# Affine part of a reloaded residual on VectorE by halves, more zero matmuls at the start, and high passes first, in a two-layer decoder trunk

## The chip, the cores and the metric

The kernel runs on one core of a Trainium2 chip. The metric is device time in microseconds (us) of one execution. The engines of the core are TensorE (PE: matmuls and transposes, and PEld, its weight load), VectorE (DVE), ScalarE (ACT) and GpSimd (POOL); SyncE (SP) issues most transfers. Matmul results land in PSUM, all else lies in SBUF.

## The reference

Input and output are 512 tokens (S) by 1024 channels (D), float32. After a first layer norm come two equal layers:

```python
for l in range(DEPTH):                       # DEPTH = 2
    proj = h @ w_in[l]
    cq, ckv, kr, xp, xqk, xv, xo, ipre, fpre = jnp.split(proj, ...)
    a = mla(cq, ckv, kr, ...)                # attention, 4 heads
    p = multiscale_pool(xp, ...)
    m = mlstm(xqk, xv, xo, ipre, fpre, ...)
    mix = jnp.concatenate([a, p, m], axis=-1) @ w_out[l]
    h = layer_norm(ALPHA * h + mix, ln1_g[l], ln1_b[l])
    f = conv_glu_ffn(h, w_up[l], w_fconv[l], b_fconv[l], w_down[l])
    h = layer_norm(ALPHA * h + f, ln2_g[l], ln2_b[l])
```

## The kernel before

**Tiles and products.** The tokens stand in NT = 4 tiles of 128, the channels in KD = 8 groups of 128 ("k-tiles"). Each float32 operand is split into a high part (rounded to fp32r) and a low part (the rest), and each product is three matmuls: hi times hi, hi times lo, lo times hi. Weights are streamed. `fetch` (L145 on) issues the transfer of one piece of at most 1024 columns into a raw buffer (of 2), lets ScalarE copy it to hi (L158) and one engine, named piece by piece in the table of `add_w`, subtract for lo (L159: VectorE or GpSimd); hi and lo have 4 buffers each. `getw` fetches at most one piece ahead of the one in use. Names carry the piece: lo_o_1_2 is the low part of quarter 2 of half 1 of w_out, and the quarters are taken in that order.

**Order.** TensorE's order is written by generators that a planner runs, each by its readiness and modelled time; the other engines' instructions are ordered by a scheduler that goes by priority.

**Opening.** x comes in by tiles. TensorE multiplies zeros (wz, L381) 14 times. `first_norm` makes each tile's statistics and normalised value, writes it to DRAM (`spill`, L230) without gain and bias, and transposes it (L239, tp_in, in two halves of four k-tiles); ScalarE applies gain and bias (L244), and `split` makes a_hi (L178) and a_lo (L179). `tm_gemm` then computes the projection ia tile by tile over six k-tiles, three matmuls (L290, L291, L292) for each in a row: x hi by weight hi, x hi by weight lo, x lo by weight hi. After it runs the remaining two k-tiles as further groups.

**Attention.** The q, k and v projections are evacuated by VectorE: qn, qp (with its rotary steps, L737 to L741, and L722), kn, v (L179). Softmax takes a maximum (L783), and pr (L789) is transposed (L806, pt). Meanwhile the lo parts of uq_1 and of all of half 0 of w_out are made on GpSimd.

**Output projection and residual.** The attention's pool is closed; `spill` is read back as h, four 128x1024 tiles, GpSimd multiplies by the gain gb_p (L885) and VectorE adds the bias (L886). w_out runs in two column halves (`out_gen`): half 0 with one chunk in its last group, half 1 with three, so that tile after tile is completed over chunks 1, 2 and 3. `resid` evacuates half a tile: h = ALPHA h + psum (L834) and its statistics (L193). After half 1 `ln_tail` normalises, writes to `spill` (in the last layer to the output), transposes and splits; the gain and bias of ln1, g1, are applied to h on GpSimd during the feed-forward part (`ln_affine`).

**Feed-forward and tail.** `t_half` runs the first three up pieces over token tiles 0 and 1, then 2 and 3; `t_one` the others. The down projection is again a `tm_gemm` in two halves, its last group three chunks long in half 1. In the last layer `ln_tail` ends in the output: subtract mean and multiply by gain (L210), multiply by rs and add bias (L224, VectorE), the last tile by halves; for tile 2 ScalarE multiplies (L212) and GpSimd adds (L217). rs comes from GpSimd's power (L190).

Of the kernel before, what the change touches and what calls it, by code (L numbers as in the profile page):

```python
# [13 lines left out]
AF = mybir.ActivationFunctionType  # L14
ALU = mybir.AluOpType
# [3 lines left out]
P = 128  # L19
# [76 lines left out]
def trunk(ctx: ExitStack, tc: tile.TileContext, I: dict, out: bass.AP, layers=DEPTH):  # L96
# [33 lines left out]
    def mmc(n):  # L130
        return n / 2400.0 + 0.003
# [66 lines left out]
    def ln_tail(pool, h, i, st, gb, cols, name, transpose=True, dst=None, pre=1.3):  # L198
# [6 lines left out]
        if not transpose:  # L205
            n = D // 2 if i == NT - 1 else D
            with ExitStack() as hs:
                if i == NT - 1:
                    hs.enter_context(tc.high_priority(offset=1000))
                V.scalar_tensor_tensor(z, z, mv[:, 0:1], gb[:, 0, :], ALU.subtract, ALU.mult)  # L210
                if i == NT - 2:
                    A.activation(z, z, AF.Copy, scale=rs[:, 0:1])  # L212
                    for a in range(0, D, D // 2):
                        if a:
                            yield 0.0, 0.0, "rs_end"
                            hs.enter_context(tc.issue_after(last_rs[0]))
                        G.tensor_add(z[:, a : a + D // 2], z[:, a : a + D // 2], gb[:, 1, a : a + D // 2])  # L217
                        A.dma_start(dst[i * P : (i + 1) * P, a : a + D // 2], z[:, a : a + D // 2])
                    return
                if i == NT - 1:  # L220
                    sch.set("rs_end")
                for a in range(0, D, n):
                    za = z[:, a : a + n]
                    V.scalar_tensor_tensor(za, za, rs[:, 0:1], gb[:, 1, a : a + n], ALU.mult, ALU.add)  # L224
                    nc.sync.dma_start(dst[i * P : (i + 1) * P, a : a + n], za)
# [34 lines left out]
    def tm_gemm(chunks, n, stat, evac, name, nlast=1, nfirst=1, waits=None, twaits=None):  # L260
# [7 lines left out]
        for g in groups:  # L268
# [11 lines left out]
            for i in range(NT):  # L280
                if twaits and done == 0:
                    yield 0.0, 0.0, twaits[i]
                at = done
                for (hi, lo), kts in loaded:
# [25 lines left out]
    def t_half(names, waits):  # L310
        ws, os_ = [], []
        for hf in range(2):
# [3 lines left out]
            for n, nm in enumerate(names):  # L316
# [5 lines left out]
                for k in range(KD):  # L322
                    mm3(os_[n][:, t0 * P : t1 * P], hi[:, k * P : (k + 1) * P], lo[:, k * P : (k + 1) * P],
                        a_hi[:, t0:t1, k, :], a_lo[:, t0:t1, k, :], k == 0, k == KD - 1)
                    if k % 2 == 1:
                        yield 6 * mmc(256), 0.0, None
# [22 lines left out]
    for l in range(layers):  # L349
# [12 lines left out]
        add_w(I["w_uq"][l, 1], 6 * P, f"uq{l}_1", G)  # L362
        for half in range(2):
            for q in range(4):
                add_w(I["w_out"][l, half, q], 1024, f"o{l}_{half}_{q}", G if half == 0 else V)
# [14 lines left out]
    for i in range(14):  # L380
        T.matmul(wp, wz[:, :P], wz, start=True, stop=True)  # L381
# [18 lines left out]
    def first_norm():  # L400
        for i in range(NT):
# [3 lines left out]
            yield from ln_tail(lp, h, i, st, None, cols0, "in0", dst=spill)  # L405

# [634 lines left out]
```

## Time and profile before

| | before |
|---|---|
| median of 3 runs | 1184.91 us (1182.11 to 1185.75) |
| the profiled execution | 1184.34 us |
| its span | 1182.5 us |
| TensorE busy | 1139.6 us, 96% |
| VectorE busy | 631.4 us, 53% |
| ScalarE busy | 471.0 us, 40% |
| GpSimd busy | 265.1 us, 22% |
| granted TensorE clock, mean | 0.987 |

The span runs from the first to the last recorded instruction. Busy time is the union of an engine's instructions. [...] Line numbers (L159) are of the kernel before, and PSUM tiles carry the name of what is computed (o: output projection).

### The profile page before, as it was taken

The numbers are of one execution on the slowest core, as the hardware profiler recorded it, in microseconds if no ns is written. First come the engines' busy times: TensorE is split into PE (matmuls) and PEld (weight loads), VectorE is DVE, ScalarE is ACT, GpSimd is POOL, SyncE is SP. The second block draws the span as 40 slices with busy tenths as digits, with TensorE's granted clock in tenths as the row PEclk, the third lists the DMA queues.
The fourth block names the chain that finished last, engine by engine and source line by source line (L and its number), as shares of the span: only waits on it lengthen the run. The fifth ranks groups of instructions, "written<-read, shape, count | busy, mean of one in ns | idle before, by whom it ended". The sixth has DMA issues, their size and how long they took to land.

```text
span 1182.5 us, 14079 instructions
## 1 busy us (share of the span) xinstructions
PE 1139.6 (96%) x5426; PEld 948.4 (80%) x5426; DVE 631.4 (53%) x975; ACT 471.0 (40%) x815; POOL 265.1 (22%) x202
## 2 busy tenths in 40 slices
PE   7999999799999999999999999979999999999996
PEld 5878878688888888888887887868888888888885
DVE  6766885754543444223368579676544533432325
ACT  6564542453333333221267545417433333331120
POOL 0316613013331111000003363040334211110002
PEclk8999999899999999999999999989999999999998
DMA  7331214233243232323243112152323433332321
GB/s 291 103 104 60 85 37 160 89 108 104 92 131 101 90 106 89 104 92 94 96 154 125 63 50 89 53 180 58 113 98 107 125 99 97 93 104 89 107 72 71
DMA packets 35074, 120.76 MB, mean 102 GB/s; under 512 B 4408, under 2 KB 4920, under 8 KB 35008
## 3 DMA queue, kind: packets, MB, share of 16 engines
q1 hardware_dynamic: 34720, 119.35, 31.3%
q8 instruction: 42, 0.69, 0.2%
q10 hardware_dynamic: 288, 0.52, 0.1%
q14 instruction: 24, 0.20, 0.1%
HBM read 113.55 MB, written 6.31 MB: 101 GB/s over the span
## 4 chain that ended last, share of the span: by engine, by line
PE 76%; DVE 13%; POOL 4%; issue 2%; ACT 2%; DMA 1%; SPq 0%; POOLq 0%; DVEq 0%; ACTq 0%
PE t_up L173 13%; PE t_up L175 13%; PE t_up L174 13%; PE d L292 6%; PE d L290 6%; PE d L291 6%; PE o L291 1%; PE o L292 1%; PE o L290 1%; PE ia L292 1%; DMA h<-spill 1%; DVE qp L722 1%; PE ia L291 1%; PE ia L290 1%; POOL py L532 1%
## 5 line engine op out<-in xcount | busy, mean ns | idle before, releaser
L173 PE MATMUL t_up<-a_hi,hi_up 128*128 128x512 f32 (+1 forms) x752 | 282.7, 376 | 0.0
L174 PE MATMUL t_up<-a_lo,hi_up 128*128 128x512 f32 (+1 forms) x752 | 282.6, 376 | 0.0
L175 PE MATMUL t_up<-a_hi,lo_up 128*128 128x512 f32 (+1 forms) x752 | 282.3, 375 | 0.0
L159 DVE TENSOR_TENSOR lo_up<-raw_up,hi_up 128x1024 fp32r<-128x1024 f32 x88 | 120.6, 1371 | 162.5 <-ACT hi_up L158 159.4
L158 ACT CAST hi_up<-raw_up 128x1024 fp32r<-128x1024 f32 x88 | 92.8, 1054 | 182.7 <-PE t_up L174 170.2
L175 PEld LDWEIGHTS t_up<-a_hi,lo_up 128*128 128x128 f32 x752 | 141.5, 188 | 25.8
L174 PEld LDWEIGHTS t_up<-a_lo,hi_up 128*128 128x128 f32 x752 | 141.5, 188 | 25.8 <-DVE a_lo L179 0.2
L173 PEld LDWEIGHTS t_up<-a_hi,hi_up 128*128 128x128 f32 x752 | 141.5, 188 | 25.3
L914 POOL TENSOR_TENSOR f_lo<-y,f_hi 128x512 fp32r<-128x512 f32 x44 | 77.4, 1760 | 366.6 <-ACT f_hi L913 366.6
L159 DVE TENSOR_TENSOR lo_d<-raw_d,hi_d 128x1024 fp32r<-128x1024 f32 x44 | 53.9, 1224 | 159.6 <-ACT hi_d L158 159.2
L290 PE MATMUL d<-hi_d,f_hi 128*128 128x512 f32 x352 | 137.1, 389 | 0.0
L292 PE MATMUL d<-hi_d,f_lo 128*128 128x512 f32 x352 | 136.9, 389 | 0.0
L291 PE MATMUL d<-lo_d,f_hi 128*128 128x512 f32 x352 | 136.9, 389 | 0.0
L158 ACT CAST hi_d<-raw_d 128x1024 fp32r<-128x1024 f32 x44 | 46.4, 1055 | 176.2 <-PE d L292 157.1
L291 PEld LDWEIGHTS d<-lo_d,f_hi 128*128 128x128 f32 x352 | 66.1, 188 | 13.8
L292 PEld LDWEIGHTS d<-hi_d,f_lo 128*128 128x128 f32 x352 | 66.1, 188 | 13.7
L290 PEld LDWEIGHTS d<-hi_d,f_hi 128*128 128x128 f32 x352 | 66.1, 188 | 13.6
L912 DVE TENSOR_TENSOR y<-y,t_up 128x512 f32<-128x512 f32 x44 | 30.3, 688 | 74.4 <-PE t_up L175 66.9
L908 ACT ACTIVATE y<-y 128x512 f32<-128x512 f32 x44 | 27.8, 632 | 101.4 <-DVE y L907 101.4
L907 DVE SCALAR_TENSOR_TENSOR y<-t_up,pp,y 128x511 f32<-128x511 f32 x88 | 65.6, 746 | 1.5
L291 PE MATMUL o<-lo_o,a_hi 128*128 128x512 f32 x128 | 52.1, 407 | 13.8 <-DVE lo_o L159 13.8
L190 POOL TENSOR_TENSOR rs_d<-rs_d,nhalf 128x1 f32<-128x1 f32 x8 | 8.3, 1036 | 233.5 <-DVE rs_d L189 233.5
(264 smaller groups left out, 1927.1 us busy)
## 6 DMA issues: line engine op xcount, KB each, us to landing
raw_up<-in_w_up_dram SPq DMA_DIRECT2D x88, 512.0 KB, 3.5
raw_d<-in_w_dn_dram SPq DMA_DIRECT2D x44, 512.0 KB, 3.4
raw_o<-in_w_out_dram SPq DMA_DIRECT2D x16, 512.0 KB, 3.5
raw_it<-in_w_it_dram SPq DMA_DIRECT2D x12, 512.0 KB, 3.4
spill<-h SPq DMA_DIRECT2D x8, 512.0 KB, 2.8
raw_ib<-in_w_ib_dram SPq DMA_DIRECT2D x8, 512.0 KB, 3.5
h<-spill SPq DMA_DIRECT2D x8, 512.0 KB, 7.5
raw_uq<-in_w_uq_dram SPq DMA_DIRECT2D x6, 384.0 KB, 3.0
```

The costliest lines, as they stand in the source:

```text
L158: A.copy(h_, r_)
L159: eng.tensor_tensor(l_, r_, h_.bitcast(F32), ALU.subtract)
L173: T.matmul(o, whi, xhi, start=start, stop=False)
L174: T.matmul(o, whi, xlo, start=False, stop=False)
L175: T.matmul(o, wlo, xhi, start=False, stop=stop)
L290: T.matmul(o, xhi, whi, start=at == 0, stop=False)
L291: T.matmul(o, xhi, wlo, start=False, stop=False)
L292: T.matmul(o, xlo, whi, start=False, stop=at == nk - 1)
L907: V.scalar_tensor_tensor(y[:, t:], o[:, : S - t], w(2 - t), y[:, t:], ALU.mult, ALU.add)
L908: A.activation(y, y, AF.Silu)
L912: V.tensor_mul(y, y, o)
L914: f_sub[0] = G.tensor_sub(fbox["lo"][:, f, :], y, fbox["hi"][:, f, :].bitcast(F32)).ins
```

## The change

Seven things, the order following the diff:

1. In the last layer all tiles' final steps are on VectorE; the last tile does both steps by halves, and its second half leaves by ScalarE's queue.
2. In `tm_gemm`, where the first group waits tile by tile (ia alone), four k-tiles at a time run all hi·hi matmuls, then all with the weight's lo, then all with a_lo.
3. `t_half` does the same by four k-tiles.
4. The lo of uq_1 and of quarters 2 and 3 of w_out's half 0 moves from GpSimd to VectorE.
5. 29 zero matmuls instead of 14, and 6 more behind the transposes of tile 0.
6. Gain and bias of the reloaded h are both applied on VectorE, by halves of 512 columns: half 0 of all tiles first, half 1 of a tile behind the evacuation of its half 0. The transfers of g1's gain and bias are asked for later.
7. The last group of the last layer's second down half has four chunks instead of three.

```diff
         if not transpose:
             n = D // 2 if i == NT - 1 else D
-            with ExitStack() as hs:
-                if i == NT - 1:
-                    hs.enter_context(tc.high_priority(offset=1000))
-                V.scalar_tensor_tensor(z, z, mv[:, 0:1], gb[:, 0, :], ALU.subtract, ALU.mult)
-                if i == NT - 2:
-                    A.activation(z, z, AF.Copy, scale=rs[:, 0:1])
-                    for a in range(0, D, D // 2):
-                        if a:
-                            yield 0.0, 0.0, "rs_end"
-                            hs.enter_context(tc.issue_after(last_rs[0]))
-                        G.tensor_add(z[:, a : a + D // 2], z[:, a : a + D // 2], gb[:, 1, a : a + D // 2])
-                        A.dma_start(dst[i * P : (i + 1) * P, a : a + D // 2], z[:, a : a + D // 2])
-                    return
-                if i == NT - 1:
-                    sch.set("rs_end")
+            with tc.high_priority(offset=1000 if i == NT - 1 else 0):
+                for a in range(0, D, n):
+                    za = z[:, a : a + n]
+                    V.scalar_tensor_tensor(za, za, mv[:, 0:1], gb[:, 0, a : a + n], ALU.subtract, ALU.mult)
                 for a in range(0, D, n):
                     za = z[:, a : a + n]
                     V.scalar_tensor_tensor(za, za, rs[:, 0:1], gb[:, 1, a : a + n], ALU.mult, ALU.add)
-                    nc.sync.dma_start(dst[i * P : (i + 1) * P, a : a + n], za)
+                    (A if a else nc.sync).dma_start(dst[i * P : (i + 1) * P, a : a + n], za)
             return
...
                     yield 0.0, 0.0, twaits[i]
                 at = done
+                if twaits and done == 0:
+                    ops = [(hi, lo, q, kt) for (hi, lo), kts in loaded for q, kt in enumerate(kts)]
+                    for a in range(0, len(ops), 4):
+                        for p_ in range(3):
+                            for hi, lo, q, kt in ops[a : a + 4]:
+                                w = (lo if p_ == 1 else hi)[:, q * 512 : q * 512 + n]
+                                T.matmul(ps[i][:, :n], stat(kt, i)[p_ == 2], w, start=a == p_ == 0 and kt == ops[0][3],
+                                         stop=False)
+                        yield 3 * len(ops[a : a + 4]) * mmc(n), 0.0, None
+                    at = len(ops)
+                    continue
...
                 hi, lo = ws[n]
-                for k in range(KD):
-                    mm3(os_[n][:, t0 * P : t1 * P], hi[:, k * P : (k + 1) * P], lo[:, k * P : (k + 1) * P],
-                        a_hi[:, t0:t1, k, :], a_lo[:, t0:t1, k, :], k == 0, k == KD - 1)
-                    if k % 2 == 1:
-                        yield 6 * mmc(256), 0.0, None
+                for k0 in range(0, KD, 4):
+                    for p_ in range(3):
+                        for k in range(k0, k0 + 4):
+                            T.matmul(os_[n][:, t0 * P : t1 * P], (lo if p_ == 1 else hi)[:, k * P : (k + 1) * P],
+                                     (a_lo if p_ == 2 else a_hi)[:, t0:t1, k, :], start=k == p_ == 0,
+                                     stop=k == KD - 1 and p_ == 2)
+                    yield 12 * mmc(256), 0.0, None
...
-        add_w(I["w_uq"][l, 1], 6 * P, f"uq{l}_1", G)
+        add_w(I["w_uq"][l, 1], 6 * P, f"uq{l}_1", V)
...
-                add_w(I["w_out"][l, half, q], 1024, f"o{l}_{half}_{q}", G if half == 0 else V)
+                add_w(I["w_out"][l, half, q], 1024, f"o{l}_{half}_{q}", G if half == 0 and q < 2 else V)
...
     wp = bank("wp")
-    for i in range(14):
-        T.matmul(wp, wz[:, :P], wz, start=True, stop=True)
+
+    def warm(n):
+        for _ in range(n):
+            T.matmul(wp, wz[:, :P], wz, start=True, stop=True)
+
+    warm(29)
...
             yield from ln_tail(lp, h, i, st, None, cols0, "in0", dst=spill)
+            if i == 0:
+                warm(6)
...
-                h, gb = hbox["h"], hbox[which]
...
                     V.scalar_tensor_tensor(z, z, ALPHA, ps, ALU.mult, ALU.add)
                     ln_stats(h, i, half, stt[i])
+                if half == 0 and which == "g1":
+                    hbox["pre"](i, 1)
                 if half == 1:
...
         for i in range(NT):
             nc.sync.dma_start(h[:, i, :], spill[i * P : (i + 1) * P, :])
-            G.tensor_mul(h[:, i, :], h[:, i, :], gp[:, 0, :])
-            V.tensor_add(h[:, i, :], h[:, i, :], gp[:, 1, :])
-        hbox.update(h=h, pool=hp, g1=load_gb(hp, I["ln1_g"][l], I["ln1_b"][l], "1"))
+
+        def pre_affine(i, half):
+            c_ = slice(half * 512, half * 512 + 512)
+            V.tensor_mul(h[:, i, c_], h[:, i, c_], gp[:, 0, c_])
+            V.tensor_add(h[:, i, c_], h[:, i, c_], gp[:, 1, c_])
+
+        for i in range(NT):
+            pre_affine(i, 0)
+        hbox.update(h=h, pool=hp, pre=pre_affine)
...
             ffn_open()
+            hbox["g1"] = load_gb(hp, I["ln1_g"][l], I["ln1_b"][l], "1")
...
-                                   f"d{half}", nlast=1 if half == 0 else 3))
```

VectorE at the junction of the output projection and the residual, first layer. The o_0 to o_3 at L834 (L842 in the new numbering) are the PSUM tiles of the four token tiles, h the reloaded residual, st_a its statistics, lo_o_1_2 and lo_o_1_3 the low weights of half 1. Before:

```order
L159 TENSOR_TENSOR lo_o_1_2_2044<-raw_o_1_2_2041,hi_o_1_2_2043 128x1024
L886 TENSOR_TENSOR h_1946<-h_1946,gb_p 128x1024 x2
L834 SCALAR_TENSOR_TENSOR h_1946<-h_1946,o_0_1694 128x512
L886 TENSOR_TENSOR h_1946<-h_1946,gb_p 128x1024
L193 BN_STATS st_a_1977<-h_1946 128x6
L834 SCALAR_TENSOR_TENSOR h_1946<-h_1946,o_1_1695 128x512
L834 SCALAR_TENSOR_TENSOR h_1946<-h_1946,o_2_1696 128x512
L193 BN_STATS st_a_1986<-h_1946 128x6
L193 BN_STATS st_a_1995<-h_1946 128x6
L834 SCALAR_TENSOR_TENSOR h_1946<-h_1946,o_3_1697 128x512
L159 TENSOR_TENSOR lo_o_1_3_2050<-raw_o_1_3_2047,hi_o_1_3_2049 128x1024
L193 BN_STATS st_a_2004<-h_1946 128x6
```

The changed kernel, the end of the same stretch:

```order
L193 BN_STATS st_a_2006<-h_1967 128x6
L899 TENSOR_TENSOR h_1967<-h_1967,gb_p 128x512
L842 SCALAR_TENSOR_TENSOR h_1967<-h_1967,o_2_1717 128x512
L898 TENSOR_TENSOR h_1967<-h_1967,gb_p 128x512
L193 BN_STATS st_a_2017<-h_1967 128x6
L899 TENSOR_TENSOR h_1967<-h_1967,gb_p 128x512
L842 SCALAR_TENSOR_TENSOR h_1967<-h_1967,o_3_1718 128x512
L898 TENSOR_TENSOR h_1967<-h_1967,gb_p 128x512
L193 BN_STATS st_a_2028<-h_1967 128x6
L899 TENSOR_TENSOR h_1967<-h_1967,gb_p 128x512
L159 TENSOR_TENSOR lo_o_1_2_2070<-raw_o_1_2_2067,hi_o_1_2_2069 128x1024
L159 TENSOR_TENSOR lo_o_1_3_2076<-raw_o_1_3_2073,hi_o_1_3_2075 128x1024
```

The low weights lo_o_1_2 and lo_o_1_3 stand together behind all multiplications (L898), additions (L899) and half-0 evacuations; before, lo_o_1_2 stood behind the first addition and lo_o_1_3 behind the last evacuation.

VectorE in the attention, first layer; the L722 rows (L730 in the new numbering) are the rotated q, and mx is the first maximum of a softmax. Before:

```order
L179 TENSOR_TENSOR v_1393<-uv_1369,v_1393 128x512
L722 TENSOR_TENSOR qp_1402<-qp_1287,qp_1402 64x512 x2
L179 TENSOR_TENSOR v_1407<-uv_1370,v_1407 128x512
L722 TENSOR_TENSOR qp_1416<-qp_1314,qp_1416 64x512 x2
L179 TENSOR_TENSOR v_1421<-uv_1371,v_1421 128x512
L179 TENSOR_TENSOR qn_1440<-uq_1_1430,qn_1440 128x512
L783 TENSOR_REDUCE mx<-s 128x1
```

The changed kernel:

```order
L179 TENSOR_TENSOR v_1414<-uv_1390,v_1414 128x512
L730 TENSOR_TENSOR qp_1423<-qp_1308,qp_1423 64x512 x2
L179 TENSOR_TENSOR v_1428<-uv_1391,v_1428 128x512
L730 TENSOR_TENSOR qp_1437<-qp_1335,qp_1437 64x512 x2
L179 TENSOR_TENSOR v_1442<-uv_1392,v_1442 128x512
L179 TENSOR_TENSOR qn_1461<-uq_1_1451,qn_1461 128x512
L159 TENSOR_TENSOR lo_o_0_2_1878<-raw_o_0_2_1875,hi_o_0_2_1877 128x1024
L791 TENSOR_REDUCE mx<-s 128x1
L159 TENSOR_TENSOR lo_o_0_3_1936<-raw_o_0_3_1933,hi_o_0_3_1935 128x1024
L792 TENSOR_SCALAR mx<-mx 128x1
```

The order of v and qp is the same; lo_o_0_2 and lo_o_0_3 come in around the first maximum. (The lo of uq_1 stands further ahead, between the two qn in front of the rotary steps.)

TensorE in the opening; ia_162 (ia_177 in the new one) is token tile 0's PSUM tile, hi_ia_0 to hi_ia_2 hold two k-tiles of the weight each, and tp_in are transposes. Before, from the transposes of tile 1 on:

```order
L239 MATMUL tp_in_200<-ident,h_92 128x128 x4
L239 MATMUL tp_in_212<-ident,h_92 128x128 x4
L290 MATMUL ia_162<-hi_ia_0_121,a_hi 128x456
L291 MATMUL ia_162<-lo_ia_0_122,a_hi 128x456
L292 MATMUL ia_162<-hi_ia_0_121,a_lo 128x456
L290 MATMUL ia_162<-hi_ia_0_121,a_hi 128x456
L291 MATMUL ia_162<-lo_ia_0_122,a_hi 128x456
L292 MATMUL ia_162<-hi_ia_0_121,a_lo 128x456
L290 MATMUL ia_162<-hi_ia_1_127,a_hi 128x456
L291 MATMUL ia_162<-lo_ia_1_128,a_hi 128x456
L292 MATMUL ia_162<-hi_ia_1_127,a_lo 128x456
```

The changed kernel, from the same transposes to those of tile 2:

```order
L228 MATMUL tp_in_221<-ident,h_92 128x128 x4
L228 MATMUL tp_in_233<-ident,h_92 128x128 x4
L279 MATMUL ia_177<-hi_ia_0_136,a_hi 128x456 x2
L279 MATMUL ia_177<-hi_ia_1_142,a_hi 128x456 x2
L279 MATMUL ia_177<-lo_ia_0_137,a_hi 128x456 x2
L279 MATMUL ia_177<-lo_ia_1_143,a_hi 128x456 x2
L279 MATMUL ia_177<-hi_ia_0_136,a_lo 128x456 x2
L279 MATMUL ia_177<-hi_ia_1_142,a_lo 128x456 x2
L279 MATMUL ia_177<-hi_ia_2_148,a_hi 128x456 x2
L279 MATMUL ia_177<-lo_ia_2_149,a_hi 128x456 x2
L279 MATMUL ia_177<-hi_ia_2_148,a_lo 128x456 x2
L228 MATMUL tp_in_273<-ident,h_92 128x128 x4
```

Where a_lo was asked for by the third matmul, it is asked for by the ninth; the last two k-tiles of the group follow as two more triples of passes.

## Rows read from the trace of the kernel before

**Rows 1.** The page's busy times: us, share of the span, instructions.
```profile
PE 1139.6 (96%) x5426; PEld 948.4 (80%) x5426; DVE 631.4 (53%) x975; ACT 471.0 (40%) x815; POOL 265.1 (22%) x202
```
**Rows 2.** TensorE's waits: who, for whom: us in total, times, longest us.
```profile
PE o L291 <- DVE lo_o L159: 13.8, 2, 6.9
...
PE s L173 <- DVE v L179: 3.4, 2, 1.7
```
**Rows 3.** Windows: us, PE, PEld, DVE, ACT, POOL busy, PEclk, DMA share, GB/s.
```profile
210.00:220.00 10.00, 5.47 (x14) 4.33 (x15) 8.37 (x14) 0.00 (x0) 0.55 (x1) 0.66 0.59 206
```
**Rows 4.** Timeline, TensorE, opening: start, us, operation, [idle before <- releaser].
```profile
1.25 4.79 PE L381 MATMUL wp<-wz 128*128 128x512 bf16 x14 [1.25 <-DVE wz L378]
9.46 1.09 PE L239 MATMUL tp_in<-ident,h 128*128 128x128 f32 x8 [3.42 <-DVE h L228]
...
13.42 0.48 PE L290 MATMUL ia<-hi_ia,a_hi 128*128 128x456 f32 x1 [1.60 <-ACT a_hi L178]
...
16.33 0.75 PE L292 MATMUL ia<-hi_ia,a_lo 128*128 128x456 f32 x1 [2.22 <-DVE a_lo L179]
...
22.12 1.03 PE L239 MATMUL tp_in<-ident,h 128*128 128x128 f32 x8
```
**Rows 5.** Timelines of ScalarE and VectorE, opening.
```profile
17.57 0.62 ACT L178 CAST a_hi<-lnt_in 128x512 fp32r<-128x512 f32 x1
...
19.53 0.64 DVE L179 TENSOR_TENSOR a_lo<-lnt_in,a_hi 128x512 fp32r<-128x512 f32 x1
```
**Rows 6.** Timeline of VectorE, attention of the first layer.
```profile
136.32 0.68 DVE L741 TENSOR_TENSOR qp<-qp,qp 128x512 f32<-128x512 f32 x1
136.92 0.69 DVE L737 TENSOR_TENSOR qp<-uq,cs 128x512 f32<-128x512 f32 x1
...
141.04 0.96 DVE L741 TENSOR_TENSOR qp<-qp,qp 128x512 f32<-128x512 f32 x1
...
145.03 3.50 DVE L722 TENSOR_TENSOR qp<-qp,qp 64x512 fp32r<-64x512 f32 x2
...
149.29 2.77 DVE L722 TENSOR_TENSOR qp<-qp,qp 64x512 fp32r<-64x512 f32 x2
```
**Rows 7.** Timeline of GpSimd, the same stretch.
```profile
145.41 2.57 POOL L159 TENSOR_TENSOR lo_o<-raw_o,hi_o 128x1024 fp32r<-128x1024 f32 x1 [3.96 <-ACT hi_o L158]
```
**Rows 8.** Timeline of TensorE, behind that stretch.
```profile
154.98 0.30 PE L806 MATMUL pt<-ident,pr 128*128 128x128 f32 x1 [0.22 <-DVE pr L789]
```
**Rows 9.** Chain of waits, 186 to 245 us: start, us on the chain, what.
```profile
187.95 6.29 DMA h<-spill
...
219.17 0.43 PE o L292
...
219.87 0.23 PE o L291
```
**Rows 10.** Timeline of VectorE, junction of the first layer.
```profile
200.16 3.41 DVE L159 TENSOR_TENSOR lo_o<-raw_o,hi_o 128x1024 fp32r<-128x1024 f32 x1
...
208.56 1.21 DVE L886 TENSOR_TENSOR h<-h,gb_p 128x1024 f32<-128x1024 f32 x1
...
213.27 1.21 DVE L159 TENSOR_TENSOR lo_o<-raw_o,hi_o 128x1024 fp32r<-128x1024 f32 x1
```
**Rows 11.** Timeline of TensorE, junction and first up projection.
```profile
214.53 0.80 PE L291 MATMUL o<-lo_o,a_hi 128*128 128x512 f32 x1 [6.85 <-DVE lo_o L159]
...
232.97 0.36 PE L173 MATMUL t_up<-a_hi,hi_up 128*128 128x256 f32 x1
```
**Rows 12.** Timelines of VectorE and GpSimd, tail.
```profile
1163.63 1.28 DVE L224 SCALAR_TENSOR_TENSOR h<-h,rs_d,gb 128x1024 f32<-128x1024 f32 x1 [0.44 <-POOL rs_d L190]
...
1174.15 0.15 DVE L189 TENSOR_SCALAR rs_d<-mv_d 128x1 f32<-128x1 f32 x1
1174.21 1.26 POOL L217 TENSOR_TENSOR h<-h,gb 128x512 f32<-128x512 f32 x1 [1.26 <-ACT h L212]
...
1177.00 2.40 DVE L224 SCALAR_TENSOR_TENSOR h<-h,rs_d,gb 128x512 f32<-128x512 f32 x2 [0.44 <-POOL rs_d L190]
```

More of the change, by code (lines that the diff above doesn't have):

```diff
@@ L826, in f @@
             def f(i, ps):
-                h, gb = hbox["h"], hbox[which]
+                h, gb = hbox["h"], hbox.get(which)
                 if half == 0:
@@ L940, in ffn_main @@
                                          dst=out if last else spill),
-                                   f"d{half}", nlast=1 if half == 0 else 3))
+                                   f"d{half}", nlast=1 if half == 0 else 4 if last else 3))
             if not last:
```

## The prediction

> **What bounds the kernel now.** The page's first part comes first: TensorE is busy 1139.6 of 1182.5 us, every other engine at most 53% [rows 1]. So the end moves only by what TensorE idles, by what it runs at the lower clock, and by what follows its last matmul. The list of TensorE's waits is next: by far the largest is for a lo weight of the output projection, 13.8 us in two waits, one a layer; 3.4 us go to the attention's v, again in two [rows 2]. The opening and the tail are read from the timelines. The profiled run took 1184.34 us, span 1182.5; the sum is made against 1184.34. The median, 1184.91, is 0.6 above it. A measurement of this kernel can tell about 0.3%, 3.5 us, from no change.
>
> **Opening.** The 14 zero matmuls take 4.79 us from 1.25 on; then TensorE idles 3.42 until the first transposes at 9.46 [rows 4]. A 512-column matmul takes 0.43 at the lower level of the clock and 0.23 at the higher one [rows 9], so 4.79 is about 8 of the first and 6 of the second. Fifteen more at 0.23 are 3.45: they end at 6.04 + 3.45 = 9.5, as the transposes become ready. If the clock rose later, 29 x 0.43 = 12.5 would end at 13.7 and hold them up. The six zeros behind tile 0's transposes (1.4 us) lie in the idle time before the first projection matmul, 1.60 long [rows 4]: no cost. Then TensorE waits again, 2.22 us for an a_lo, until 16.33, and that matmul takes 0.75 where the first one at 13.42 took 0.48 [rows 4]: the clock has fallen. With all hi passes of four k-tiles first, eight matmuls run before the first a_lo is asked for, so most of the 2.22 goes. What is late next is the data of tile 0's other half: a_hi at 17.57 + 0.62 = 18.2, a_lo at 19.53 + 0.64 = 20.2 [rows 5], and behind it two matmuls, some 20.6 where before the tile ended at 22.12 [rows 4]. That is 1.5; I take **-1.2**, as tile 1's halves follow closely. Bounds: -1.5, and +1.4 for zeros that stay at the lower clock and hold up the six behind them. The same reordering in the first three up tiles alters no wait that the trace shows: 0.
>
> **Attention, each layer.** VectorE multiplies 128x512 fp32 tiles at 0.60 from start to start (136.32 to 136.92), but two 64x512 ones took 3.50 together [rows 6], while GpSimd worked on a lo_o at 145.41, 2.57 long [rows 7]; another follows it. TensorE waits 1.7 for what stands behind them [rows 2]. The change takes two lo_o from GpSimd: this pair and the next should cost 0.65 each, some 3.6 us less. It puts on VectorE the lo of uq_1, 768 columns at 1.21 / 1024 [rows 10], 0.9, ahead of the qp chain, and behind it two lo_o at 1.15, which the first softmax meets: 3.2 in all. So v comes earlier and the softmax hardly: the transposes of pr start at 154.98 now, with 0.22 of waiting [rows 8], and are late next. I take **-0.3** a layer, -0.6 in two; bounds -0.8 (half of the wait for v) and +1.0 (one lo_o uncovered) each.
>
> **The junction of output projection and residual, each layer.** h comes back from DRAM, issued at 187.95 and 6.29 later there [rows 9]. Then GpSimd multiplies, VectorE adds. While GpSimd runs, VectorE's lo_o_1_2 takes 3.41 instead of 1.21, and lo_o_1_3 stands last, behind four adds and four evacuations; it is done at 214.48 [rows 10]. TensorE has idled 6.85 by 214.53 [rows 11], and works at 0.66 of the clock over 210 to 220 [rows 3].
>
> After, GpSimd has nothing here, and VectorE's row is, by order: 16 multiplications and additions of 128x512, 4 evacuations, 4 statistics, then lo_o_1_2, lo_o_1_3. At 0.60 each, 24 are 14.4 us; from 187.95 + 6.29 = 194.24 on they end at 208.7, lo_o_1_2 at 209.9. I take 210.3, for the dependent pairs in the row. TensorE asks for lo_o_1_2 after the first matmul on that chunk, six matmuls of 0.23 earlier than it now stops: 214.53 - 6.85 = 207.68, less 1.4, is 206.3. So the stall is 4.0 instead of 6.85. At its end 11 matmuls of tile 0 are to do instead of 5, 1.4 us of work moved behind the stall; 210.3 answers to 211.7 in the old row: 214.5 - 211.7 = 2.8 gained. Then the clock: twelve matmuls at 0.43 instead of 0.23 cost 2.4 now [rows 9]; behind a shorter stall I take two thirds, 0.8 gained. **-3.6** a layer, -7.2 in two. Bounds: the 24 at 0.68, the duration itself, are 1.9 later (-1.7; with the full clock loss -1.2); no fall of the clock at all is another 1.6 to 1.9 gained (-5.5). On SP, g1's gain now stands ahead of raw_up_0_0 and waits until the last addition has read gb_p, 208.7: raw_up_0_0 leaves at 209.1 instead of about 203.6. Its lo is wanted at 232.97 [rows 11], 14 us behind its landing and split even if TensorE is 3 us earlier; nothing else queued there is due sooner: 0.
>
> [...] Two independent instructions start 0.60 apart, though each lasts 0.68 [rows 6]: the second starts before the first is done. [...] The rows decide for independent neighbours; for the additions behind their multiplications no row here is that pair.
>
> **Tail.** rs_d is asked of GpSimd at 1174.15 + 0.15, but GpSimd adds until 1174.21 + 1.26 = 1175.47, and then makes the power: 1.1 late [rows 12]. The last two halves take 2.40, beside GpSimd's second addition; a whole row of the same 1024 elements without it took 1.28 [rows 12]: 1.1. Both additions go: -2.2, what is late next is the power itself, alone on its queue. Tile 2 costs VectorE one step of 1.28 more [rows 12], but with four chunks in the last group the tiles end 24 matmuls apart instead of 18, 6 x 0.23 = 1.4 further, so its steps are out of the last tile's way. Those four chunks must be split 6 matmuls earlier than three, and their four buffers of hi and lo are all held by one group; the list of waits has none for lo_d: 0, and as a bound 1.4 lost. The last half's DMA leaves from ScalarE's queue, idle there: 0, or some tenths gained. **-2.2**; bounds -2.4, and +0.3 if the halves stay slow (-1.1) and the 1.4 is lost.
>
> **Sum.** -1.2 - 0.6 - 7.2 - 2.2 = -11.2: 1184.34 - 11.2 = 1173.1. Bounds taken together: best -1.5 - 1.6 - 11.0 - 2.4 = -16.5, 1167.8; worst +1.4 + 2.0 - 2.4 + 0.3 = +1.3, 1185.6.
>
> **The rivals.**
> (a) *No fall of the clock* after a stall of 4 us. For it: 3.42 idle before 9.46 did not leave the transposes slow. Against it: the matmul at 16.33 is slow behind waits of 1.60 and 2.22 [rows 4]. It gains another 1.8 a layer: 1173.1 - 3.6 = 1169.5.
> (b) *Each of the 24 costs its full duration.* 24 x 0.08 = 1.9 a layer, 3.8: 1176.9. [...] For it: the dependent pairs; against it: the starts in rows 6.
> (c) *The attention gets later*: the qp pair is slow for a reason of its own, and 3.2 us come on top, 3 a layer, 6: 1179.1. For it: the first of the kind overlaps GpSimd only in part; against it: a multiplication that GpSimd touched took 0.96, its neighbours 0.68 [rows 6].
> (d) *Slower.* VectorE becomes the bound at the junction, because a 128x512 step there costs 0.96, as L741 at 141.04 did [rows 6], the transfers of four tiles and the weights coming into SBUF at the same time. 24 x 0.36 = 8.6 a layer, 17.3 in two: 1190.4. It decides from 0.60 + 11.2 / 48 = 0.83 a step. Against it: the only addition of 1024 elements here without GpSimd beside it took 1.21 [rows 10].
> (e) *The change moves idle time and no more*: what is gained at the junction is lost at the first softmax and in the opening, 1183 to 1186.
>
> **How the numbers follow.** My sum 0.52; (a) 0.16; (b) 0.11; (c) 0.08; (d) 0.05; (e) 0.08. The predicted time is that of the sum, 1173. The range leaves out (d), (e) and a little at the bottom and reaches to (a)'s and (c)'s times with a margin of the opening's bound: 1167.5 to 1180.5. Faster by over 0.3% (below 1181): the sum, (a), (b), (c), 0.87. Within 0.3%: (e), 0.08. Slower: (d), 0.05.
>
> **What the new profile would show.** TensorE's wait for lo_o should be about 4 us a layer, lo_o_1_2 ending near 210 less what came earlier; steps of L898 and L899 start 0.60 apart. The wait for v should be gone or have become one for pr. In the opening no wait of 2 us for a_lo and no slow stretch; in the tail rs_d 0.15 behind its VectorE step and the last two halves in about 1.3. The prediction is wrong if L898 steps take over 0.8, if the first softmax stands more than 1 us later, or if the shorter stall leaves as long a slow stretch as the long one.

## The result: 0.9936 of the time before, and the profile after

Median of 8 runs 1177.07 us (1171.50 to 1178.66), before 1184.34 (8 runs): ratio 0.9936, interval 0.9919 to 0.9952. That is 7.3 us less; 11.2 were forecast, and the range, 1167.5 to 1180.5, holds the time. The profiled execution took 1175.83 us, its span is 1174.0 against 1182.5: 8.5 less.

The first line of the page, and TensorE's three longest waits (who, for whom: us in total, times, longest us), of the changed kernel:

```profile
PE 1142.0 (97%) x5447; PEld 948.4 (81%) x5447; DVE 626.9 (53%) x1007; ACT 469.0 (40%) x814; POOL 225.3 (19%) x186
```

```profile
PE o L291 <- DVE lo_o L159: 8.6, 2, 5.1
PE cols L602 <- ACT mr L597: 3.6, 2, 2.0
PE pt L814 <- DVE pr L797: 2.9, 2, 1.5
```

Against [rows 2] the wait for lo_o fell from 13.8 to 8.6, the wait for v is gone, and one for pr has come. The second line is new in the reading: cols <- mr was 2.1 before, nearly all of it in layer 0.

Where the time went shows best in TensorE itself. Its matmuls are the same but for the zeros and for their order in parts 2, 3 and 7, so the start of a matmul can be set against that of the same matmul before. Starts from the timelines of each profiled execution, minus those of the kernel before, in us (e1 to e10 are the experiments below):

| matmul (start before) | changed | e1 tail | e2 junction | e3 lo | e4 opening | e9 no zeros | e10 no high passes |
|---|---|---|---|---|---|---|---|
| transposes of tile 2 (22.12) | -1.78 | +0.39 | -0.21 | +0.16 | -1.60 | -1.60 | -1.21 |
| first mLSTM sums, layer 0 (92.19) | -2.69 | +0.37 | -0.20 | +0.17 | -2.52 | -1.08 | -2.78 |
| first matmul on v, layer 0 (162.46) | -1.99 | +0.36 | -0.22 | -0.71 | -0.82 | -0.52 | -3.63 |
| first up, layer 0 (232.97) | -6.08 | +0.54 | -4.64 | -0.53 | -1.92 | -4.74 | -8.02 |
| first it, layer 1 (619.31) | -6.29 | +0.53 | -4.65 | -0.52 | -2.17 | -4.97 | -8.06 |
| first mLSTM sums, layer 1 (669.05) | -3.62 | +0.54 | -4.64 | -0.49 | +0.49 | -3.96 | -8.04 |
| first matmul on v, layer 1 (739.29) | -4.46 | +0.58 | -4.65 | -0.02 | +0.49 | -4.80 | -7.40 |
| first up, layer 1 (809.87) | -6.10 | +0.72 | -8.55 | +0.12 | +1.02 | -8.83 | -9.38 |
| last down (1171.96) | -6.11 | +0.72 | -8.57 | +0.11 | +1.02 | -8.84 | -9.39 |
| end of the span (1182.55) | -8.58 | -1.75 | -8.58 | +0.12 | +1.01 | -11.31 | -11.86 |

The column of the changed kernel reads: 1.8 gained in the opening, 0.9 in layer 0's mLSTM stretch, 0.7 lost in its attention, 4.1 gained at its junction; then 2.7 lost in layer 1's mLSTM stretch, 0.8 gained in its attention, only 1.6 at its junction, 2.5 in the tail. Each column is one execution, and the clock does not do the same in each: the 8 runs of the changed kernel lie between 1171.50 us, at a mean granted clock (a share of TensorE's full speed) of 0.994, and 1178.66 us, at 0.989. Stretches that a part does not touch differ by up to 0.5 between most columns, and by 1.5 or more where the clock fell in one trace and not in the other (1.7 in e4's attention). The opening of before is in e1, at +0.39 at tile 2's transposes, and also in e12, at -1.37. So a step of under some 1.5 us in one column is not by itself the kernel's.

**Junction.** VectorE and TensorE there (timelines: start, us, operation, idle before and releaser), layer 0 and then layer 1:

```profile
192.13 1.29 DVE L898 TENSOR_TENSOR h<-h,gb_p 128x512 f32<-128x512 f32 x2 [3.31 <-DMA h<-spill]
...
206.54 2.35 DVE L159 TENSOR_TENSOR lo_o<-raw_o,hi_o 128x1024 fp32r<-128x1024 f32 x2
...
768.11 1.29 DVE L898 TENSOR_TENSOR h<-h,gb_p 128x512 f32<-128x512 f32 x2 [4.94 <-DMA h<-spill]
...
782.51 2.35 DVE L159 TENSOR_TENSOR lo_o<-raw_o,hi_o 128x1024 fp32r<-128x1024 f32 x2
```

```profile
207.81 0.50 PE L291 MATMUL o<-lo_o,a_hi 128*128 128x512 f32 x1 [3.48 <-DVE lo_o L159]
...
783.78 0.80 PE L291 MATMUL o<-lo_o,a_hi 128*128 128x512 f32 x1 [5.10 <-DVE lo_o L159]
```

The 24 steps run from 192.13 to 206.54, 14.41 us, 0.60 each, and 14.40 in layer 1; the stall answers to [rows 11]. In layer 1 the row begins 1.6 us later behind the issue of h: 760.32 to 768.11 is 7.8, 185.96 to 192.13 is 6.2.

The clock, in windows (us, then PE, PEld, DVE, ACT, POOL busy, PEclk, DMA share, GB/s) behind the two junctions, in layer 0's attention and in layer 1's mLSTM stretch; the lower level is a PEclk of 0.50, the full clock 1.00:

```profile
208.90:212.30 3.40, 3.40 (x10) 2.66 (x9) 0.31 (x1) 0.00 (x0) 0.00 (x0) 0.50 0.74 259
782.40:789.20 6.80, 5.42 (x13) 4.26 (x14) 2.78 (x4) 1.05 (x1) 0.00 (x0) 0.50 0.73 283
154.30:157.70 3.40, 3.40 (x18) 3.02 (x17) 3.30 (x14) 1.39 (x6) 0.00 (x0) 0.50 0.04 11
635.60:639.00 3.40, 3.40 (x6) 1.68 (x5) 2.29 (x4) 2.38 (x4) 0.00 (x0) 0.50 0.44 172
```

It is at the lower level for half as long at the first junction (3.4 us) as at the second (6.8), where the first 1.4 us lie still in the stall. The other two stretches were at full clock before (1.00 over 154 to 162 and over 630 to 645). The one of [rows 4] in the opening, at 0.50 over 14.8 to 21.5 before, is gone, and so is one in layer 0's mLSTM stretch, which the kernel before had:

```profile
62.60:66.00 3.40, 3.40 (x6) 1.67 (x5) 2.61 (x5) 2.52 (x5) 0.00 (x0) 0.51 0.74 265
```

### The profile page after: what moved, and what is told of

It is laid out like the page before. It is cut to its first block, busy times and chain, and to the rows that moved or that the text cites. A ratio compares the mean times of both kernels' runs of the same rounds, so it can differ in the third digit from the quotient of the medians.

```text
span 1174.0 us, 14137 instructions
## 1 busy us (share of the span) xinstructions
PE 1142.0 (97%) x5447; PEld 948.4 (81%) x5447; DVE 626.9 (53%) x1007; ACT 469.0 (40%) x814; POOL 225.3 (19%) x186
## 5 line engine op out<-in xcount | busy, mean ns | idle before, releaser
L173 PE MATMUL t_up<-a_hi,hi_up 128*128 128x512 f32 x656 | 255.2, 389 | 0.0
L174 PE MATMUL t_up<-a_lo,hi_up 128*128 128x512 f32 x656 | 255.2, 389 | 0.0
L175 PE MATMUL t_up<-a_hi,lo_up 128*128 128x512 f32 x656 | 255.2, 389 | 0.0
L173 PEld LDWEIGHTS t_up<-a_hi,hi_up 128*128 128x128 f32 x656 | 123.1, 188 | 25.6
L175 PEld LDWEIGHTS t_up<-a_hi,lo_up 128*128 128x128 f32 x656 | 123.1, 188 | 25.5
L174 PEld LDWEIGHTS t_up<-a_lo,hi_up 128*128 128x128 f32 x656 | 123.1, 188 | 25.5
L292 PEld LDWEIGHTS d<-hi_d,f_lo 128*128 128x128 f32 x352 | 66.1, 188 | 13.8
```

Source lines behind the costliest of these rows:

```text
L173: T.matmul(o, whi, xhi, start=start, stop=False)
L174: T.matmul(o, whi, xlo, start=False, stop=False)
L175: T.matmul(o, wlo, xhi, start=False, stop=stop)
L292: T.matmul(o, xlo, whi, start=False, stop=at == nk - 1)
```

## Experiments: each part alone

All medians below are of 4 to 10 runs, each with its ratio to the kernel before on the same chip. The lines shown are from one execution of each.

**e1, parts 1 and 7 (tail).**

> The kernel before with parts 1 and 7 of the change alone (last tiles on VectorE only, four chunks in the last group). Theory A, each part is worth what its own stage shows: TensorE's last matmul stands where it stood before (1172 after the span's start), the span ends 2.4 us earlier, as in the changed kernel, whose span from the last matmul's start to the end is 2.4 shorter; time -2.2 to -2.4, some 1182. Theory B, the tail is worth more in company: less than 1.2 here.

1180.37, ratio 0.9974 (0.9962 to 0.9987). From the start of the last matmul to the end the span is 8.12 us, before 10.59: 2.5 less, as in the changed kernel. Theory A. The rows that answer to [rows 12] (VectorE's timeline):

```profile
1174.80 0.15 DVE L189 TENSOR_SCALAR rs_d<-mv_d 128x1 f32<-128x1 f32 x1
1174.87 1.40 DVE L210 SCALAR_TENSOR_TENSOR h<-h,mv_d,gb 128x512 f32<-128x512 f32 x2
1176.19 1.41 DVE L213 SCALAR_TENSOR_TENSOR h<-h,rs_d,gb 128x512 f32<-128x512 f32 x2
```

From rs_d's step to the last two halves are now 1.4 us, before 2.85 (1174.15 to 1177.00); the halves take 1.41 instead of 2.40.

**e2, part 6 (junction).**

> The kernel before with part 6 alone (gain and bias of the reloaded h on VectorE by halves). Theory A (the stall is the length of VectorE's row of 24 steps, and the clock's fall is decided by what TensorE did just before): both stalls for lo_o fall from 6.9 to 3.5 to 5.1, and the shift of TensorE against before over each junction is between -1.6 (clock low as long as before) and -4.1 (half as long); together -3.3 to -8.2, the span some 1174 to 1179. Theory B (the changed kernel's second junction gained only 1.6 because of something the other parts did ahead of it): here both junctions gain the same, about -4.1 each.

1175.78, ratio 0.9934 (0.9914 to 0.9955). Both junctions gain alike, 4.4 and 3.9 (table: -0.22 to -4.64, -4.65 to -8.55). So nearly the whole gain is this part's, and something that the other parts bring takes 2.3 away in the second one: theory B. TensorE's stall there and the clock behind it:

```profile
782.24 0.63 PE L291 MATMUL o<-lo_o,a_hi 128*128 128x512 f32 x1 [3.73 <-DVE lo_o L159]
```

```profile
782.50:785.90 3.40, 3.40 (x9) 2.63 (x9) 0.82 (x1) 0.00 (x0) 0.00 (x0) 0.50 0.82 260
```

3.73 instead of 5.10, and half as long at the lower clock.

**e3, part 4 (lo on VectorE).**

> The kernel before with part 4 alone (lo of uq_1 and of two quarters of w_out on VectorE). Theory A: the wait for v (1.7 a layer) goes, the first softmax waits instead, TensorE's shift behind the attention is -0.3 to -1.2 a layer unless the clock falls there (then up to +0.7); time -2.4 to +1.4. Theory B (the qp steps are slow for a reason of their own): the pairs at L722 stay at 3.5 and 2.8 us and the attention is 3 us later a layer, +6.

1183.93, ratio 0.9997 (0.9981 to 1.0012). The qp pairs take 1.41 and 1.40 us, against 3.50 and 2.77 in [rows 6]; GpSimd was the cause. TensorE now waits for the softmax instead (timeline):

```profile
154.78 0.30 PE L806 MATMUL pt<-ident,pr 128*128 128x128 f32 x1 [1.44 <-DVE pr L789]
155.90 0.41 PE L806 MATMUL pt<-ident,pr 128*128 128x128 f32 x2 [0.82 <-DVE mx L784]
```

2.3 us of waiting against 2.7 before (1.69 for v, then 0.22, 0.68 and 0.16 for the softmax). TensorE's shift over the attention is -0.9 in layer 0 (+0.17 to -0.71) and +0.5 in layer 1, where the clock fell behind the waits: no gain, theory A.

**e4, parts 2, 3 and 5 (opening).**

> The kernel before with parts 2, 3 and 5 (zeros, high passes first). Theory A (the scheduler's new order of VectorE in the mLSTM stretch comes with the high passes of the first group): tile 2's transposes 1.8 earlier; the wait of the cols transposes for mr in layer 0 no longer than before, and in layer 1 about 2 us instead of 0.3, with a stretch at the lower clock behind it; the gain at the end is then 0 to 1 us, not 1.8. Theory B (that wait comes from the earlier arrival of TensorE after the other parts): the wait in layer 1 is under 0.5 us and the 1.8 reach the end.

1184.58, ratio 1.0008 (0.9997 to 1.0020): nothing gained. The opening's 1.6 are there, 2.5 by the first mLSTM sums. In the attention 1.7 go: its longest wait, 1.68 for v, is as long as before, but the clock is at 0.5 over 151.7 to 158.5, where it was at 1.0 before. Then 2.7 go in layer 1's mLSTM stretch. There TensorE waits 2.00 where it waited 0.3 before (cols holds transposes of gate rows of the mLSTM part; mr and fr are two of these rows, and c is the output of its convolution):

```profile
638.69 0.22 PE L613 MATMUL cols<-ident,mr 4*128 4x4 f32 x1 [2.00 <-ACT mr L608]
```

Why, VectorE's timeline shows, before and then in e4:

```profile
635.74 2.28 DVE L510 TENSOR_TENSOR c<-c,th 128x512 f32<-128x512 f32 x1
637.94 0.67 DVE L583 TENSOR_TENSOR fr<-fr,mr 4x512 f32<-4x512 f32 x1
...
634.44 2.28 DVE L529 TENSOR_TENSOR c<-c,th 128x512 f32<-128x512 f32 x1
636.64 0.74 DVE L525 SCALAR_TENSOR_TENSOR c<-t_it,pp,c 128x511 f32<-128x511 f32 x1
637.30 0.67 DVE L602 TENSOR_TENSOR fr<-fr,mr 4x512 f32<-4x512 f32 x1
```

A conv step (L525) stands ahead of fr - mr; before, in layer 1, it stood behind. ScalarE's exponential overwrites mr and must wait until fr - mr has read it, and the transposes of cols wait for the exponential. That step accounts for 0.66 of the 1.7 us. The other 1.0 comes from ScalarE, whose order moved too: a copy for a weight's high part now stands ahead of the first conv step there, and VectorE's row follows that step. Before, and then in e4:

```profile
627.94 0.79 ACT L504 ACTIVATE c<-t_it,pp 128x512 f32<-128x512 f32 x1
...
628.98 1.07 ACT L158 CAST hi_ib<-raw_ib 128x1024 fp32r<-128x1024 f32 x1
...
625.68 1.07 ACT L158 CAST hi_ib<-raw_ib 128x1024 fp32r<-128x1024 f32 x1
626.63 0.80 ACT L523 ACTIVATE c<-t_it,pp 128x512 f32<-128x512 f32 x1
```

This conv step comes 1.3 us earlier than before, TensorE reaches cols 2.3 us earlier. So the scheduler's order moved in a stretch that no part of the change touches. In layer 0 the conv step and fr - mr change places the other way round, and the wait goes from 1.76 to 1.56.

The wait itself costs about 1 us in layer 1, and the rest of the 2.7 is the lower clock, which does not always follow it: e5, e7 and e9 below have the same wait (1.98 to 2.05), the clock stays up behind it, and the stretch loses 1.0 (e9 in the table: -4.97 to -3.96).

## Experiments: what was given back

**e10, the changed kernel without part 2; e9, without part 5.** The first asks whose the order is, the second why h lands late in layer 1.

> The changed kernel without part 2: the first projection group takes its three matmuls per k-tile in a row again. Theory A (part 2 alone brings VectorE's new order in the mLSTM stretch): the wait for mr in layer 1 is 0.3 instead of 2.0 and no lower clock follows it, so TensorE's shift there stays where it was (-6 instead of -3.6), and in layer 0 the wait is 1.8 with the lower clock at 62 back (+0.9); the opening loses 0.5 to 1.5; together -1.5 to +0.5 against the changed kernel. Theory B (the wait comes with an early TensorE): the wait in layer 1 stays at 2 us and the time is 1 us or more above the changed kernel. In both the landing of h in layer 1 stays at 7.4 to 7.8, since the zeros are in.

1174.08, ratio 0.9929 (0.9907 to 0.9952). The wait for mr in layer 1 is 0.3 us:

```profile
631.26 0.22 PE L591 MATMUL cols<-ident,mr 4*128 4x4 f32 x1 [0.33 <-ACT mr L586]
```

and TensorE loses nothing there (-8.06 to -8.04). Theory A: without part 2 that order is gone, and e9 shows that it comes without part 5 too. In this pair of traces part 2 gained 0.6 at tile 2's transposes (-1.78 against -1.21) and cost 2.7 later. One forecast missed: in layer 0 the old order and the wait are back (1.84), but the lower clock is not, and that stretch gains 1.6 (-1.21 to -2.78). In e5 and e9 it falls there with the new order. So the 0.9 gained there by the changed kernel is not shown to come from the order. In the time itself e10 and the changed kernel do not differ clearly (0.9929 and 0.9936, with overlapping intervals).

> The changed kernel without part 5: 14 zero matmuls as before, none behind tile 0's transposes. The reloaded h of layer 1 landed 7.4 to 7.8 us behind its issue in every kernel with the 21 further zero matmuls, and 6.3 to 6.6 in every kernel without them; in the former a packet of the instruction queue (16 KB, 0.93 us) falls into that transfer, 5 us behind the issue, in the latter it comes 9 us behind it. Theory A (the zeros move TensorE's code, and with it the packet): without them tile 0 of h lands in 6.3 to 6.6 us in layer 1, the stall there is 3.5 to 3.8 instead of 5.1, the lower clock behind it lasts 3.4 instead of 6.8, and TensorE's shift over the second junction against the kernel before is -3.9 instead of -1.6. In the opening up to 1.5 us are lost, since the clock falls there. Theory B (the landing is later because of the time at which TensorE comes, or chance): 7.4 to 7.8 as before.

1172.99, ratio 0.9923 (0.9896 to 0.9950). The landing of the reloaded h in layer 1 (view of the tile: issue to landing, least, median, most), in the changed kernel and then in e9:

```profile
DMA to landing us min/median/max: 7.7/8.8/9.7
```

```profile
DMA to landing us min/median/max: 6.2/7.4/9.4
```

The DMA view between the issue of tile 0 and its landing has, in the changed kernel (packets, MB, share):

```profile
q1 hardware_dynamic: 655, 2.43, 97.1%
q8 instruction: 1, 0.02, 0.8%
```

and in e9 only

```profile
q1 hardware_dynamic: 520, 1.93, 82.6%
```

The two transfers of gb_p ahead of h land alike, 2.90 and 5.08 behind the issue of h in the changed kernel, 2.81 and 4.92 in e9. Without the zeros the packet of the instruction queue comes 8.6 us behind the issue, with them 5.4. Over all kernels: with the packet 8.4 to 8.9 us behind (before, e1, e2, e3, e9, e11, e12) tile 0 landed in 6.2 to 6.6 us; with it 4.5 to 5.4 behind (changed, e4, e5, e6, e8, e10) in 7.4 to 7.8; in e7, which has 14 more zeros ahead, it came 1.6 before the issue, inside gb_p's transfer, and h landed in 7.5. Theory A, for the packet and the landing; that the packet carries TensorE's code no view shows. The stall in e9 is 3.64 and the lower clock 3.4 long, and the second junction gains 4.0 (-4.80 to -8.83), as in e2. In the time itself e9 and the changed kernel do not differ clearly (0.9923 and 0.9936). The opening lost less than was forecast: tile 2's transposes stand at -1.60 instead of -1.78, though the clock was at its lower level for 6.8 us from 14.4 on; 1.4 more are gone by the first mLSTM sums, with a fall of the clock at 62. The packet, of 0.02 MB, stands between gb_p and h, and the stall is 1.1 to 1.5 us longer with it (4.79 to 5.15 in the changed kernel, e6 and e10; 3.64 and 3.73 in e9 and e2).

**e6, the exponential in a tile of its own.**

```diff
+            er = mix.tile([MH, S], F32, name="er")
-            A.activation(mr, mr, AF.Exp, scale=-1.0)
+            A.activation(er, mr, AF.Exp, scale=-1.0)
```

(and the transposes read er).

> The changed kernel with the exponential of -mr written to a tile of its own instead of over mr, so that ScalarE need not wait until VectorE's fr - mr has read mr. Theory A (the cols transposes wait because VectorE's order, new with the high passes, puts a conv step ahead of fr - mr): the waits of 1.6 and 2.0 us for mr go in both layers, and the lower clock at 635.6 in layer 1 with them; -1.6 in layer 0, -2 to -4 in layer 1, time some 1170 to 1173. Theory B (TensorE only arrives earlier at the next thing that is late): less than 1 us is gained.

1174.62, ratio 0.9911 (0.9896 to 0.9926). The wait for mr is gone; what is late next is the conv's own result, in layer 0 and 1:

```profile
63.46 1.13 PE L617 MATMUL mq<-c,wbd 128*128 128x512 f32 x2 [1.28 <-DVE c L518]
...
635.84 1.12 PE L617 MATMUL mq<-c,wbd 128*128 128x512 f32 x2 [0.96 <-DVE c L518]
```

Layer 0 gains nothing by it (theory B). Against the trace of the changed kernel layer 1 gains 2.0 (from -1.41 at 613 to -3.42 at 665), with the fall of the clock away. But the clock stayed up in e5, e7 and e9 too, which lack this edit, and against their 1.0 the stretch loses 0.65 here: of the 2.0 some 0.4 is the edit's. The time does not differ clearly from that of the changed kernel (0.9911 and 0.9936, with overlapping intervals): nearer to theory B.

**e7, zeros in the stall.**

```diff
                         T.matmul(o, xhi, whi, start=at == 0, stop=False)
+                        if name == "o1" and i == 0 and at == 4:
+                            for _ in range(14):
+                                T.matmul(o, zz[:, :P], zz, start=False, stop=False)
```

> The changed kernel with 14 zero matmuls added into tile 0's sum ahead of the first matmul on lo_o_1_2, that is into the stall, 3.2 us at the higher clock. Theory A (the clock falls behind the stall because TensorE idled in it): no stretch at the lower clock behind the first junction, -1.7 there; in the second, with a stall of 3.5 to 5.1, -1.7 to -3.4; lo_o itself comes no earlier. Theory B (the clock falls there whatever TensorE does): the stretches at 0.5 stay as long and the time is the changed kernel's.

1172.66, ratio 0.9895 (0.9880 to 0.9909). Windows behind the two junctions:

```profile
207.60:211.00 3.40, 2.66 (x12) 1.83 (x11) 2.37 (x3) 0.00 (x0) 0.00 (x0) 1.00 0.56 153
782.80:786.20 3.40, 3.40 (x10) 2.63 (x9) 0.22 (x2) 0.08 (x1) 0.00 (x0) 0.50 0.91 317
```

In layer 0 the clock does not fall, and 1.3 us are gained (+0.79 to -0.55 against the changed kernel). In layer 1 the zeros fill 3.2 us, 2.3 of waiting remain, and the lower clock lasts 3.4 instead of 6.8; 0.6 gained. Theory A at these two junctions: with a wait of 0.7 us left in layer 0 the clock stayed at 1.00, with the 3.48 of the changed kernel it fell. Another 1.7 of this trace's gain is that the clock did not fall behind the wait for mr, which the edit does not touch.

**e5, lo_o_1_2 and lo_o_1_3 first.**

```diff
-        eng.tensor_tensor(l_, r_, h_.bitcast(F32), ALU.subtract)
+        with tc.high_priority(offset=2000 if name[:1] == "o" and name[-4:] in ("_1_2", "_1_3") else 0):
+            eng.tensor_tensor(l_, r_, h_.bitcast(F32), ALU.subtract)
```

> The changed kernel with the subtraction for lo_o_1_2 and lo_o_1_3 at a higher priority, so that lo_o_1_2 stands behind the third of VectorE's 24 steps and lo_o_1_3 behind the eleventh. Theory A (TensorE waits for the place of lo_o in VectorE's row and for nothing else there): both waits of 3.5 to 5.1 us for lo_o go, and with them the two stretches at the lower clock (1.7 to 3.4 us); TensorE's shift over the two junctions is -11 to -14 against the changed kernel; time some 1164 to 1167. Theory B (the evacuations of h, now later, are waited for instead): the wait moves to tile 0's transposes or to PSUM banks, and less than 4 us are gained.

1170.10, ratio 0.9870 (0.9854 to 0.9886). TensorE no longer waits for lo_o. The next late thing is tile 0's normalised h, at the end of the same VectorE row:

```profile
214.74 1.09 PE L229 MATMUL tp_a<-ident,h 128*128 128x128 f32 x8 [1.92 <-DVE h L218]
...
785.99 1.69 PE L229 MATMUL tp_a<-ident,h 128*128 128x128 f32 x8 [3.73 <-DVE h L218]
```

The two junctions gain 3.2 and 2.3 us against the changed kernel, not 11 to 14: the place of lo_o was the stall (A), the row as a whole is nearly as late (B).

**e8, e11, e12: both edits, then without part 5, then without parts 5 and 2.**

> Both edits, lo_o first and the exponential's own tile. Theory A (the two act in different stages): the sum of both, -14 to -19 against the changed kernel, some 1158 to 1163. Theory B (what is gained at one stage is waited for in the next): no better than the better of the two alone.

1169.95, ratio 0.9866 (0.9849 to 0.9882): no better than e5; theory B, as far as e6 alone had anything to add. Its span is 5.7 shorter than the changed kernel's, e5's 5.3.

> Lo first and the exponential's own tile as in the run with both, without part 5 (the further zeros). Theory A (the zeros cost the second junction its early landing, and the opening gains little from them): h of layer 1 lands 6.2 to 6.6 behind its issue instead of 7.4, TensorE's wait for tile 0's normalised h there is 2 us instead of 3.3 and its clock falls for no longer; 1 to 3 us faster than the run with both, some 1167. Theory B (lo first has taken the landing off the path): the time is that of the run with both, 1170.

1168.84, ratio 0.9861 (0.9845 to 0.9877). h lands in 6.3 us and the second wait for tp_a is 2.2 at most, as A says; but in this execution the clock fell for 3.4 behind the first, 1.7 lost. The time does not decide.

> As the last, and without part 2 (high passes first) too: of the opening only the order in the first three up pieces is left. Theory A (part 2 gains 1.2 us in the opening and, with the exponential in a tile of its own, costs nothing later): 1 to 1.5 us slower than the run before it. Theory B (its gain is given back in any case): the same time within 0.5 us.

1165.88, ratio 0.9841 (0.9826 to 0.9856), the fastest of all: against A, which had it slower. Its waits at the junctions:

```profile
PE tp_a L229 <- DVE h L218: 6.7, 4, 2.3
```

Waits of 2.17 and 2.28 there left the clock up, where e11's 1.97 in layer 0 did not. All four runs of e12 are below all four of e11. Both of the opening's edits can go, so far as these runs tell.

## Why the prediction was right in sum, and where it was not

**Junction (-3.6 a layer; -4.1 and -1.6, alone -4.4 and -3.9).** The main term and its working held. The row was to be 14.4 long and was 14.41; the stall was to be 4.0 and was 3.48, with h landing 6.05 behind its issue instead of 6.29 and lo_o_1_2 without the margin of 0.4. The clock was to give 0.8 and did in layer 0: it fell, but about eight matmuls ran at 0.43 instead of twelve, 4 x 0.2. Rival (b), the full duration for each of 24 steps, is out: 14.41 and not 16.3, with 0.60 from start to start at 0.68 each. The step that failed is "6.29 later there" for both layers: in layer 1, with the further zeros, a packet of the instruction queue lay in the transfer (5.4 us behind the issue, in e9 8.6), tile 0 landed in 7.67, the stall became 5.1 and the clock stayed low as long as before, 6.8 us, which is the third of the prediction's own signs of being wrong. Nothing of that is in the sum. (Its bound of -1.2 for the long row with the full clock loss should be -0.9 by its own terms, -1.7 + 0.8.)

**Opening (-1.2; -1.8 where it was read, +0.9 at the end when alone).** In this trace what was worked out in place was right: no fall of the clock, the a_lo of tile 0's second half late next (it ends at 19.14 + 0.64 = 19.78; the line below names the step behind it on VectorE). The bound of +1.4 was too small by its own terms, since zeros that end at 13.7 hold up by 4.2 the transposes that stood at 9.46; it did not come to that, the 29 zeros ended at 9.1. TensorE there:

```profile
13.25 1.09 PE L279 MATMUL ia<-hi_ia,a_hi 128*128 128x456 f32 x4 [0.92 <-ACT a_hi L178]
...
19.83 0.68 PE L279 MATMUL ia<-hi_ia,a_lo 128*128 128x456 f32 x2 [0.91 <-DVE rs_in L189]
20.34 1.03 PE L228 MATMUL tp_in<-ident,h 128*128 128x128 f32 x8
```

20.34 was forecast as 20.6. How much of the 1.8 is the edits' stays open: e5, with the whole opening, has -0.82 there, and e12, with the opening of before, -1.37. What failed is the silent step from there to the end: that 1.2 us gained at 22 are 1.2 us gained at 1180. VectorE's order moved in the mLSTM stretches of both layers and ScalarE's in layer 1; the prediction looked only where the diff does.

**Attention (-0.3 a layer; +0.7 and -0.8, alone -0.9 and +0.5).** The mechanism was right: v comes in time, the softmax is late next. That the clock can fall behind the two waits was not in the term. They are the same in every trace with part 4 and in both layers (1.44 to 1.49 and 0.81 or 0.82). Where the clock stayed up behind them the attention came out at -0.8 to -0.9, where it fell at +0.5 to +0.8. The changed kernel's trace has one of each, and -0.3 lies between.

**Tail (-2.2; -2.5).** Right in both halves: from rs_d's step to the last two halves 1.46 are gained, where 1.1 were forecast for the power's late start, and the halves take 1.41 and not 2.40, 1.0 for 1.1. Not in the sum: in the changed kernel the power itself takes 0.99 instead of 1.53.

**Rivals.** (a) does not hold: the clock fell at both stalls. Of (c) nothing is seen, since the qp pairs are at 1.4. (d) is out, no step took more than 0.69. (e), gains that are given back, happened for the opening, but at the mLSTM stretch and at h's landing, not at the softmax's waits.

Without the two losses, 2.7 and 2.3, the profiled execution would be 5 us shorter than it is, and 2.3 shorter than the sum. That the time came as near as it did is partly luck: against these losses stand gains that were not in the sum either, 0.9 in layer 0's mLSTM stretch, 0.6 in the opening, 0.5 at the first junction and 0.3 in the tail, while the two attentions came to -0.1 instead of -0.6.

## What to carry to other kernels

When a scheduler sets the order, read its new order in the stretches that the diff does not name, above all short chains that feed TensorE: a gain ahead of them may be given back there. A stall can cost twice, once for its length and once for the lower clock behind it (at the first junction 3.48 us and then 3.4 us at 0.50); moving what is waited for up its engine's row took the wait for it away, until the end of the row was late (in e5 1.92 and 3.73 for h instead of 3.48 and 5.10 for lo_o). Behind waits of 0.8 to 2.3 us the clock fell in some traces and not in others: before a loss or a gain is put down to an edit, look whether the clock did the same in both traces. Where an engine's row began on a landing, a landing in 7.4 to 7.8 us instead of 6.2 to 6.6 came with a stall 1.1 to 1.5 us longer.

## What the runs showed of the hardware

- In layer 1, where a packet of the instruction queue (16 KB, 0.93 us long) came 4.5 to 5.4 us behind the issue of h, the first 512 KB tile landed in 7.4 to 7.8 us; where it came 8.4 to 8.9 behind, in 6.2 to 6.6. The changed kernel and e9 differ by 21 zero matmuls at the start of the program, and some 750 us later the packet came 5.4 behind in the one and 8.6 in the other. In the kernels without these zeros it falls into the fourth tile's transfer, which landed in 9.4 to 9.5 (before, e2, e9, e11, e12); in layer 0, where no packet is, the fourth landed in 8.0 to 8.5.
- With waits for lo_o of 3.46 to 3.73 us (the first junction of the changed kernel and of e2, the second of e2 and e9) came 3.4 us at a PEclk of 0.50, with those of 5.10 (changed) and of 6.85 and 6.91 (before) 6.8, part of it within the wait; where zeros filled all but 0.7 us of one (e7) it stayed at 1.00. Behind the wait of 2.0 us for mr in layer 1 it fell in the changed kernel and e4 (3.4 us at 0.50), and stayed up in e5, e7 and e9.
- VectorE's 128x512 float32 steps start 0.60 apart and last 0.68, over 24 in a row, with no GpSimd work beside them (changed kernel, 192.13 to 206.54); beside GpSimd a 64x512 pair took 3.50 (before), without it 1.41 (e3).
